# A list scheduler's order for a two-layer hybrid decoder: a table of leads by kind of work, and a model of TensorE's clock and of VectorE's waits for GpSimd

## The chip, the cores and the metric

One core of a Trainium2 chip runs the whole program. The time is device microseconds of one execution. The engines are TensorE (PE; its weight loads are shown apart as PEld), VectorE (DVE), ScalarE (ACT), GpSimd (POOL) and SyncE (SP), which issues the DMAs here. Each engine takes its instructions in a fixed order and waits on semaphores for the others.

## The reference

Two layers of a decoder trunk on 256 tokens of width 1024, all in float32:

```
for l in range(2):
    x = x + 0.5 * swiglu(rms_norm(x, ...), ...)        # 1024 -> 2816 -> 1024
    p = rms_norm(x, mix_norm[l]) @ w_in[l]             # columns split among three mixers
    ya = dsa_attention(...)       # indexer picks 64 of 256 keys per query, softmax over them
    yb = rwkv7_time_mix(...)      # delta-rule recurrence, 4 heads of 64
    yc = gated_deltanet(...)      # chunked gated delta rule, 4 heads of 64
    x = x + concat[ya, yb, yc] @ w_out[l]
    x = x + 0.5 * swiglu(rms_norm(x, ...), ...)
```

The weights are read once from HBM, some 180 MB.

## The kernel before

**Numbers.** A float32 product is made of three TensorE products of a rounded type: each weight tile `raw` (128x1024) comes by one DMA, ScalarE copies it to `hi`, VectorE subtracts to get `lo`, and the activations are split the same way (`xh`, `xl`; `hth`, `htl`; `yh`, `yl`). The products hi·hi, hi·lo and lo·hi add up in one PSUM bank `mm`. These are the *stream*; 2816-wide feed-forward parts and the projections consist of it. A *block* here is the run of matmuls that one weight unit gives one bank (6 of 512 columns, or 12 or 24 of 256). The mixers' own products are plain float32, are small, and go through banks called `tp` (and `po`). There are 8 PSUM banks in all, 6 of which may be `mm`; 3 `raw`, 7 `hi` and 7 `lo` buffers.

**Stages of a layer.** First feed-forward part; norm of both row tiles of 128 tokens (`norm`, L203: square on ScalarE, power on GpSimd, scaling `xn` on VectorE, transposes `tp<-per,xn` on TensorE, split to `xh`, `xl`); the mixers; the output projection (`down`, L227, whose last operands are `yh0`, `yl0` from the attention, while `yh1`, `yl1` come from the other two mixers); second feed-forward part.

**The mixers.** The projection's blocks (stream) feed three mixers, which run interleaved. The names that matter below: RWKV's `tile(t)` (L600) makes for each row tile and head one bank `tp<-ar,bk` (four matmul records of 64x256), of which VectorE makes `mb` (left half, L614) and `mk` (right half, L616): 16 such evictions in a layer, and a bank comes free only when both have been read. `inverse` (L390) inverts triangular matrices of 128 by steps on 32x32 blocks: `tp<-S,Mb` and `tp<-X,ST`, 64 records each, with an eviction to `X`, `S` or `ST` on VectorE or ScalarE behind each. `hb1` is RWKV's shifted projection, `vv` the delta net's convolution and `vm` the value residual of layer 1. `index` (L980) is attention's choice of keys (`wk`, `m8`), `soft` (L1036) its softmax, `o0` and `o1` are its outputs, and `y_out` (L477) transposes outputs and splits them to `yh`, `yl`.

**What sets the order.** The functions above do not emit the program. They only log it. `Plan` (L1152) cuts the log into groups (a block is one, a single instruction of the other engines is one), works out what depends on what, and gives each group a priority: its *tail*, the length of the longest chain from its start to the program's end, in estimated durations (`cost`, L1161) and hand-over times (`HOP`, L1132). `run` (L1278) then plays the program through: among all groups whose inputs are there and whose buffers are free, it takes the one that could start soonest, over all engines, and among those of one engine that could start at the same moment the one with the longest tail. The order in which groups are taken is the order in which `emit` writes them, on every engine. Nothing in the plan is a time on the chip; the engines start when their semaphores allow. SP's order of DMAs is fixed by the log.

Of the kernel before, what the change touches and what calls it, by code (L numbers as in the profile page):

```python
# [11 lines left out]
F32R = mybir.dt.float32r  # L12
AF = mybir.ActivationFunctionType
OP = mybir.AluOpType
# [3 lines left out]
D = 1024  # L18
# [75 lines left out]
class Log:  # L94
    def __init__(self, log, nc, engine):
        self.log, self.nc, self.engine = log, nc, engine
# [1033 lines left out]

PE, ACT, DVE, POOL, SP = [getattr(mybir.EngineType, n) for n in ("PE", "Activation", "DVE", "Pool", "SP")]
HOP = {PE: 210.0, ACT: 130.0, DVE: 115.0, POOL: 70.0, SP: 0.0}  # L1132
OWN = {PE: 0.0, ACT: 123.0, DVE: 104.0, POOL: 60.0, SP: 0.0}


# [12 lines left out]
def _cols(ap):  # L1148
    return math.prod(n for _, n in list(ap.ap)[1:])


class Plan:  # L1152
    def __init__(self, log, made, bias=lambda i: 0.0):
        self.log, self.made = log, made
        self.ins = [e[4] for e in log]
        self.eng = [i.engine for i in self.ins]
        self.graph()
        self.bundle()
        self.run([x + bias(k) for k, x in enumerate(self.tail)])

    def cost(self, i):  # L1161
        kind, e = type(i).__name__, i.engine
        aps = [a for a in list(i.outs) + list(i.ins) if hasattr(a, "bass_ap")]
        n = max(_cols(a) for a in aps)
        if kind == "InstDMACopy":
            return 400.0
        if e == PE:
            m = i.ins[0]
            n = _cols(m)
            if m.dtype == F32R:  # L1170
                return n * 0.4545
            if i.is_transpose:
                return n * 0.84
            k = list(m.ap)[0][1]
            return {32: 28.0, 64: max(107.0, n * 1.0)}.get(k, max(205.0, n * 1.67))
        if e == ACT:
            return 80.0 + n * 0.85 + 60.0 * (len(aps) > 2) + 200.0 * (len(aps) > 4) + 130.0 * (len(aps) == 3 and i.func == AF.Square)
        if e == POOL:
            if kind == "InstMemset":
                return 90.0 + n * 0.83  # L1180
            return 350.0 + n * 165.0 if getattr(i, "op", None) == OP.pow else 200.0 + n * 2.3
        fast = kind == "InstTensorScalarPtr" and len(aps) == 2
        slow = kind == "InstTensorScalarPtr" and len(aps) == 4
        if n == 129:
            return 600.0
        return 80.0 + 80.0 * (kind == "InstMax") + n * (0.52 if fast else 1.05) + 60.0 * slow

    def graph(self):
        hist, masks = {}, {}
        N = len(self.ins)  # L1190
        self.pred = [set() for _ in range(N)]
# [33 lines left out]
    def bundle(self):  # L1225
        N, last = len(self.ins), None
        node, group, same = [0] * N, [], None
        for k, i in enumerate(self.ins):
            key = None
            if self.eng[k] == PE:  # L1230
                key = [self.pair.get(a.bass_ap.tensor.name) for a in i.ins]
                key = max(x or "" for x in key)
                ap = i.outs[0].bass_ap
                to = (ap.tensor.name, ap.offset) if any(self.made[a.bass_ap.tensor.name][2] == "c1040" and a.dtype == F32R for a in i.ins) else None
            if key is not None and (key == last or to and to == same):
                group[-1].append(k)
            else:
                group.append([k])
                same = to if key is not None else None
            if key is not None and same != to:  # L1240
                same = None
            last = key
            node[k] = len(group) - 1
        self.group = group
        one = lambda l: [l[g[0]] for g in group]
        self.pred = [{node[p] for k in g for p in self.pred[k]} - {n} for n, g in enumerate(group)]
        self.dur = [sum(self.dur[k] for k in g) + (80.0 if self.eng[g[0]] == PE and not (self.ins[g[0]].ins[0].dtype == F32R) else 0.0) for g in group]
        self.use = [list(dict.fromkeys(u for k in g for u in self.use[k])) for g in group]
        self.left = {}
        for l in self.use:  # L1250
            for u in l:
                self.left[u] = self.left.get(u, 0) + 1
        self.eng, self.bytes = one(self.eng), one(self.bytes)
        self.table = [getattr(self.ins[g[0]], "func", None) for g in group]
        self.table = [None if f in (None, AF.Copy, AF.Square, AF.Relu, AF.Abs) else f == AF.Silu for f in self.table]
        N = len(group)

        sp = [k for k in range(N) if self.eng[k] == SP]
        for a, b in zip(sp, sp[1:]):
            self.pred[b].add(a)  # L1260
        for k in range(N):
            back = k - 1
            if back > 0 and (not self.pred[k] and self.eng[k] == POOL or
                             self.table[k] is not None and all(self.bytes[p] for p in self.pred[k])):
                self.pred[k].add(next(j for j in range(back, -1, -1) if self.eng[j] in (PE, ACT, DVE) or not j))
        self.succ = [[] for _ in range(N)]
        for k in range(N):
            for p in self.pred[k]:
                self.succ[p].append(k)
        self.tail = [0.0] * N  # L1270
        for k in reversed(range(N)):
            e, m = self.eng[k], 0.0
            for s in self.succ[k]:
                hop = 2300.0 + self.bytes[k] / 200.0 if self.bytes[k] > self.bytes[s] else OWN[e] if self.eng[s] == e else HOP[e]
                m = max(m, self.tail[s] + hop)
            self.tail[k] = m + self.dur[k]

    def run(self, prio):  # L1278
        N = len(self.eng)
        free = dict.fromkeys(HOP, 0.0)  # L1280
        ready = {e: [] for e in HOP}
        deg = [len(p) for p in self.pred]
        at = [0.0] * N
        kinds = lambda u: [self.made[u][2]] + (["mm"] if u[:3] == "mm_" else [])
# [7 lines left out]
        for _ in range(N):  # L1292
            best = None
            for e in HOP:
                for k in ready[e]:
                    t = max(free[e], at[k], fetch if many[k] > 7 else 0.0)
                    need = [g for u in self.use[k] if u not in self.slot for g in kinds(u)]
                    for g in set(need):
                        n = need.count(g)
                        t = max(t, sorted(spare[g])[n - 1][0] if n <= len(spare[g]) else math.inf)  # L1300
                    if self.table[k] not in (None, table):
                        t += 1300.0
                    c = (t, -prio[k], k)
                    if t < math.inf and (best is None or c[0] < best[0] or (c < best and self.eng[best[2]] == e)):
                        best = c
            assert best, "the plan is stuck"
            t, _, k = best
            e = self.eng[k]
            ready[e].remove(k)
            self.order.append(k)  # L1310
            table = table if self.table[k] is None else self.table[k]
            self.begin[k] = t
            for u in self.use[k]:
                if u not in self.slot:
                    self.slot[u] = [min(spare[g]) for g in kinds(u)]
                    for g, s in zip(kinds(u), self.slot[u]):
                        spare[g].remove(s)
            end = free[e] = t + self.dur[k]
            if many[k]:
                fetch = t + 60.0 * many[k]  # L1320
            if self.bytes[k]:
                dma = max(dma, t + 2300.0) + self.bytes[k] / 290.0
                end = dma
            for u in self.use[k]:
                left[u] -= 1
                if not left[u]:
                    for g, s in zip(kinds(u), self.slot[u]):
                        spare[g].append((end + HOP[e], s[1]))
            for s in self.succ[k]:
                at[s] = max(at[s], free[e] if self.bytes[s] and self.bytes[k] else end + (HOP[e] if self.eng[s] != e else OWN[e]))  # L1330
                deg[s] -= 1
                if not deg[s]:
                    ready[self.eng[s]].append(s)
        self.time = max(free.values())


    def emit(self, tc, dram):
# [118 lines left out]
```

## Time and profile before

| | |
|---|---|
| median of 3 runs | 1176.62 us (1176.09 to 1180.11) |
| profiled execution, its own time | 1178.08 us |
| its span, first to last instruction | 1176.3 us, 22847 instructions |
| busy: DVE, ACT, POOL | 764.2, 560.7, 114.7 us |
| mean granted TensorE clock | 0.978 |
| stages in the profiled span, about | layer 0: feed-forward 7 to 202, mixers and output projection 202 to 394, feed-forward to 587; layer 1: feed-forward to 776, mixers and output projection to 981, feed-forward to 1176 |

All instructions carry the line of `emit` (L1362), so the profile is read by tile names, not by lines. Buffers that several tiles share show as `c` in the profile and as `c` with a buffer's number in the order below. A matmul's end is modelled, so a busy TensorE may still be waiting in part, or run at half its clock; the column PEclk of the view by windows gives the granted clock in each stretch.

### The profile page before, as it was taken

Reading aid. Unit: us, or ns where it says so; the run is one execution under the profiler, and the core shown is the slowest. Engines: PE = TensorE matmul, PEld = TensorE weight load, DVE = VectorE, ACT = ScalarE, POOL = GpSimd, SP = SyncE. Lnnn points to the kernel's source line nnn. Section 1 sums busy time; section 2 is a strip of 40 time slices with the busy share of each in tenths; the row PEclk is TensorE's granted clock in tenths of the full one; section 3 lists DMA queues with packets and bytes.
Section 4 is the critical chain, followed back from the end, with each engine's and each line's share of the span. In section 5 each row is a group of like instructions: output and inputs, shape, how many; then the busy total and the mean of one; then the engine's idle time right before and its main releaser. Section 6 shows DMA issues by size and latency. Waiting matters only on the chain.

```text
span 1176.3 us, 22847 instructions
## 1 busy us (share of the span) xinstructions
PE 1134.6 (96%) x9508; PEld 1013.2 (86%) x9508; DVE 764.2 (65%) x1278; ACT 560.7 (48%) x855; POOL 114.7 (10%) x137
## 2 busy tenths in 40 slices
PE   7999999999998999999999999999699989999998
PEld 5999887987787799988889998879577877999887
DVE  5676545798786657664666674558957956576543
ACT  5554434565545445443454444447435454454431
POOL 0000001153141000000000000003321410000000
PEclk9999999999899999999999999999888999999999
DMA  7766556633232466655476665644321314666561
GB/s 235 222 194 192 183 193 192 179 107 94 73 96 67 118 205 180 183 193 189 152 218 177 191 185 191 214 134 144 96 86 38 109 54 127 197 182 192 183 194 56
DMA packets 96998, 182.76 MB, mean 155 GB/s; under 512 B 9856, under 2 KB 36608, under 8 KB 96896
## 3 DMA queue, kind: packets, MB, share of 16 engines
q1 hardware_dynamic: 96752, 181.25, 51.2%
q8 instruction: 74, 1.21, 0.4%
q14 instruction: 28, 0.23, 0.1%
q10 hardware_dynamic: 144, 0.07, 0.0%
HBM read 180.25 MB, written 1.05 MB: 154 GB/s over the span
## 4 chain that ended last, share of the span: by engine, by line
PE 82%; DVE 10%; ACT 4%; issue 1%; DMA 1%; POOL 0%; SPq 0%; ACTq 0%; DVEq 0%; POOLq 0%
PE mm L1362 75%; PE tp L1362 7%; DVE c L1362 5%; DVE lo L1362 2%; ACT s L1362 1%; ACT hi L1362 1%; ACT c L1362 1%; PE po L1362 1%; DVE hb L1362 1%; DMA gb<-in_ffn_norm 0%; DMA raw<-in_w_in 0%; DVE s L1362 0%; POOL c L1362 0%; ACT xh L1362 0%; DVE bdt L1362 0%
## 5 line engine op out<-in xcount | busy, mean ns | idle before, releaser
L1362 DVE TENSOR_TENSOR lo<-raw,hi 128x1024 fp32r<-128x1024 f32 (+2 forms) x332 | 407.5, 1228 | 303.0 <-ACT hi L1362 302.1
L1362 ACT CAST hi<-raw 128x1024 fp32r<-128x1024 f32 (+2 forms) x332 | 347.1, 1047 | 412.7 <-PE mm L1362 341.8
L1362 PE MATMUL mm<-xh,hi 128*128 128x256 f32 x1360 | 384.6, 283 | 0.0
L1362 PE MATMUL mm<-xh,lo 128*128 128x256 f32 x1360 | 382.9, 282 | 0.8 <-DVE lo L1362 0.8
L1362 PE MATMUL mm<-xl,hi 128*128 128x256 f32 x1360 | 382.6, 281 | 0.0
L1362 PEld LDWEIGHTS mm<-xh,hi 128*128 128x128 f32 x1360 | 256.4, 189 | 1.9 <-issue 1.0
L1362 PEld LDWEIGHTS mm<-xl,hi 128*128 128x128 f32 x1360 | 256.6, 189 | 0.8 <-issue 0.2
L1362 PEld LDWEIGHTS mm<-xh,lo 128*128 128x128 f32 x1360 | 256.2, 188 | 1.2 <-DVE lo L1362 1.2
L1362 PE MATMUL mm<-hi,htl 128*128 128x512 f32 x352 | 138.7, 394 | 0.0
L1362 PE MATMUL mm<-lo,hth 128*128 128x512 f32 x352 | 138.5, 393 | 0.0
L1362 PE MATMUL mm<-hi,hth 128*128 128x512 f32 x352 | 138.4, 393 | 0.0
L1362 POOL TENSOR_TENSOR c<-c,per 128x256 f32<-128x256 f32 (+7 forms) x66 | 67.9, 1042 | 433.1 <-DVE c L1362 346.6
L1362 PE MATMUL mm<-hi,xh 128*128 128x512 f32 (+2 forms) x256 | 103.5, 404 | 0.7 <-ACT xh L1362 0.4
L1362 PE MATMUL mm<-hi,xl 128*128 128x512 f32 (+2 forms) x256 | 99.0, 387 | 4.9 <-DVE xl L1362 4.9
L1362 PE MATMUL mm<-lo,xh 128*128 128x512 f32 (+2 forms) x256 | 98.5, 385 | 0.5 <-DVE lo L1362 0.5
L1362 PEld LDWEIGHTS mm<-hi,htl 128*128 128x128 f32 x352 | 66.0, 188 | 15.4
L1362 PEld LDWEIGHTS mm<-lo,hth 128*128 128x128 f32 x352 | 66.1, 188 | 15.0
L1362 PEld LDWEIGHTS mm<-hi,hth 128*128 128x128 f32 x352 | 66.2, 188 | 14.8
L1362 PEld LDWEIGHTS mm<-hi,xl 128*128 128x128 f32 x256 | 50.6, 198 | 15.7 <-DVE xl L1362 6.7
L1362 PEld LDWEIGHTS tp<-c,c 32*32 32x32 f32 (+2 forms) x2328 | 41.2, 118 | 25.7 <-issue 19.8
L1362 PE MATMUL tp<-c,c 32*32 32x32 f32 (+3 forms) x2328 | 50.5, 210 | 11.3 <-DVE mk L1362 8.7
L1362 PEld LDWEIGHTS mm<-hi,xh 128*128 128x128 f32 x256 | 51.0, 199 | 11.6 <-issue 1.7
(160 smaller groups left out, 1137.3 us busy)
## 6 DMA issues: line engine op xcount, KB each, us to landing
raw<-in_ffn_w_gate SPq DMA_DIRECT2D x88, 512.0 KB, 3.8
raw<-in_ffn_w_up SPq DMA_DIRECT2D x88, 512.0 KB, 3.8
raw<-in_ffn_w_down SPq DMA_DIRECT2D x88, 512.0 KB, 3.6
raw<-in_w_in SPq DMA_DIRECT2D x46, 512.0 KB, 3.8
raw<-in_w_out SPq DMA_DIRECT2D x16, 512.0 KB, 3.4
gb<-in_ffn_norm SPq DMA_DIRECT2D x4, 512.0 KB, 4.5
raw<-in_w_in SPq DMA_DIRECT2D x4, 384.0 KB, 6.7
pp<-in_params SPq DMA_DIRECT2D x2, 729.5 KB, 6.8
```

What stands on the lines that cost most here:

```text
L1362: ins = getattr(getattr(nc, engine), op)(*map(real, a), **{n: real(x) for n, x in kw.items()}).ins
```

## The change

The reference's arithmetic, the log and the dependences stay as they are: 3144 groups before and after, and SP's order is the same in every place. What changes is how `run` chooses:

- A table `AHEAD` of 159 kinds of group (named by the tiles written and read) is added to the tail, in the plan's microseconds: `"mk0<-tp,per": 4.1` lets such a group go as if its chain were 4.1 us longer.
- An engine no longer takes only the group that could start soonest: all that could start within `SOON` of that (150 ns on PE, 200 on ACT, 100 on DVE and POOL) compete by priority.
- A model of TensorE's clock: windows of 3413 ns, beginning at a fixed phase of 0 from the plan's start, in which matmul activity is added up; after a window with too little (0.18 of full activity when warm, 0.25 when cold) the next runs at 0.53 of the speed.
- VectorE's one-input forms (`fast`) wait in the plan until GpSimd is done; other forms do not.
- 120 ns when TensorE goes from the stream to a plain float32 product, and a higher cost for wide GpSimd work.

```diff
+SOON = {PE: 150.0, ACT: 200.0, DVE: 100.0, POOL: 100.0, SP: 0.0}
+AHEAD = {
+    "D<-mb0": -7.0, "D<-mb1": -4.7, "D<-mg0": -1.9, "D<-mg1": 0.2, "Mb<-D,per": -11.6, "S64<-": 2.2, "S64<-S": -35.0,
...
+WINDOW, COLD, WARM, PHASE = 3413.0, 0.25, 0.18, 0.0
...
-        self.run([x + bias(k) for k, x in enumerate(self.tail)])
+        self.run([x + 1e3 * AHEAD.get(self.kind(k), 0.0) for k, x in enumerate(self.tail)])
...
+        def clock(t):
+            w = int((t + PHASE) // WINDOW)
+            while len(warm) <= w:
+                warm.append(used.get(len(warm) - 1, 0.0) >= (COLD if warm[-1] else WARM))
+            return w, warm[w]
...
+                    if e == PE and was and not self.stream[k]:
+                        t += 120.0
+                    if self.fast[k] and free[POOL] - pool < t:
+                        t = max(t, free[POOL])
...
-                    c = (t, -prio[k], k)
-                    if t < math.inf and (best is None or c[0] < best[0] or (c < best and self.eng[best[2]] == e)):
+                    if t < math.inf:
+                        can.append((t, -prio[k], k))
+                if can:
+                    soon = min(can)[0] + SOON[e]
+                    c = min((c for c in can if c[0] <= soon), key=lambda c: c[1:])
+                    if best is None or c[0] < best[0]:
                         best = c
```

At another place in their engine's order than before stand 305 of 644 groups on PE, 398 of 794 on ACT, 86 of 133 on POOL and 724 of 1214 on DVE, moved by at most 42 places. Three places show what moved.

**VectorE, layer 1, RWKV's evictions.** Before, these rows stand between the last but one `mb` of the second row tile and its last; `c_7_769` is `vv`, `c_8_802` its tanh:

```order
L1362 SCALAR_TENSOR_TENSOR hb_7449<-pb_7128,pp_1558,hb_7449 128x256
L1362 SCALAR_TENSOR_TENSOR c_7_769<-c_0_273,c_3_3738,c_7_769 128x256 x4
L1362 TENSOR_TENSOR lo_105<-raw_72,hi_100 128x1024
L1362 SCALAR_TENSOR_TENSOR c_7_769<-c_0_273,c_3_3738,c_7_769 128x256 x2
L1362 TENSOR_TENSOR lo_217<-raw_69,hi_209 128x1024
L1362 TENSOR_TENSOR vm<-per_61,hb_7449 128x512
L1362 SCALAR_TENSOR_TENSOR c_7_769<-c_8_802,c_7_769 128x512
L1362 TENSOR_TENSOR lo_169<-raw_67,hi_156 128x1024
L1362 TENSOR_TENSOR mk_7968<-tp,per_61 128x256 x4
```

Now all evictions of both row tiles stand in one run, with one weight split among them:

```order
L1457 SCALAR_TENSOR_TENSOR mb_7854<-tp,c_7_1897,per_61 128x256 x2
L1457 TENSOR_TENSOR mk_7872<-tp,per_61 128x256
L1457 SCALAR_TENSOR_TENSOR mb_7854<-tp,c_7_1897,per_61 128x256
L1457 TENSOR_TENSOR mk_7872<-tp,per_61 128x256 x2
L1457 SCALAR_TENSOR_TENSOR mb_7854<-tp,c_7_1897,per_61 128x256
L1457 SCALAR_TENSOR_TENSOR mb_7888<-tp,c_7_1897,per_61 128x256
L1457 TENSOR_TENSOR mk_7872<-tp,per_61 128x256
L1457 SCALAR_TENSOR_TENSOR mb_7888<-tp,c_7_1897,per_61 128x256
L1457 TENSOR_TENSOR mk_7907<-tp,per_61 128x256 x2
L1457 SCALAR_TENSOR_TENSOR mb_7888<-tp,c_7_1897,per_61 128x256
L1457 TENSOR_TENSOR lo_196<-raw_67,hi_187 128x1024
```

The rows of `hb`, `vv`, `vm` and the splits that stood ahead of the first `mk` now come behind the evictions, among the steps of `inverse`.

**TensorE, layer 1, end of the mixers.** `yh_9235` and `yl_9247` are the other mixers' operands of the output projection, `yh_9433` and `yl_9435` attention's, and `c_5_566` is attention's output of row tile 0. Before:

```order
L1362 MATMUL mm<-hi_209,yh_9235 128x512
L1362 MATMUL mm<-lo_217,yh_9235 128x512
L1362 MATMUL mm<-hi_209,yl_9247 128x512
L1362 MATMUL tp<-per_61,c_5_566 128x128 x4
L1362 MATMUL mm<-hi_156,yh_9433 128x512
L1362 MATMUL mm<-lo_169,yh_9433 128x512
```

Now (`c_6_767` and `c_8_802` are attention's two outputs, `yh_9213` the other mixers' operand):

```order
L1457 MATMUL tp<-per_61,c_5_2367 128x128 x2
L1457 MATMUL tp<-per_61,c_6_767 128x128 x4
L1457 MATMUL tp<-per_61,c_8_802 128x128 x4
L1457 MATMUL mm<-hi_107,yh_9213 128x512
L1457 MATMUL mm<-lo_118,yh_9213 128x512
L1457 MATMUL mm<-hi_107,yl_9223 128x512
```

Before, attention's output of row tile 0 is transposed right ahead of the blocks that need it. Now the last block of the other mixers' operand (12 matmuls) stands between; in layer 0 this place is as before.

**TensorE, start of the program.** The transposes of the second row tile's `xn`, and the second weight unit's block (`hi_107`, `lo_118`). Before:

```order
L1362 MATMUL mm<-hi_107,xh_96 128x512
L1362 MATMUL mm<-lo_118,xh_96 128x512
L1362 MATMUL mm<-hi_107,xl_102 128x512
L1362 MATMUL tp<-per_61,xn 128x128 x8
L1362 MATMUL tp<-c_1_149,per_61 128x128
L1362 MATMUL mm<-hi_135,xh_96 128x512
```

Now:

```order
L1457 MATMUL mm<-hi_98,xh_96 128x512
L1457 MATMUL mm<-lo_105,xh_96 128x512
L1457 MATMUL mm<-hi_98,xl_100 128x512
L1457 MATMUL tp<-per_61,xn 128x128 x8
L1457 MATMUL mm<-hi_107,xh_96 128x512
L1457 MATMUL mm<-lo_118,xh_96 128x512
```

The block of the second unit went from ahead of these transposes to behind them.

More of the change, by code (lines that the diff above doesn't have):

```diff
@@ L1132 @@
 HOP = {PE: 210.0, ACT: 130.0, DVE: 115.0, POOL: 70.0, SP: 0.0}
+SOON = {PE: 150.0, ACT: 200.0, DVE: 100.0, POOL: 100.0, SP: 0.0}
+AHEAD = {
+    "D<-mb0": -7.0, "D<-mb1": -4.7, "D<-mg0": -1.9, "D<-mg1": 0.2, "Mb<-D,per": -11.6, "S64<-": 2.2, "S64<-S": -35.0,
+    "S64<-tp": 4.1, "S<-ST": -0.5, "ST<-D,per": 0.7, "ST<-tp": -1.2, "X<-tp": 24.4, "X<-tp,per": -3.0,
+    "ar<-kx,cc": 0.4, "ast<-ast": -12.1, "ba<-mm": -19.0, "bdt<-ST": -1.3, "bdt<-tp": -0.7, "bk<-bk,e1": 17.8,
+    "bk<-kx,e1": -11.5, "bk<-kx,wa": 0.2, "cc<-cc": 19.1, "cc<-wa,cc,per": 37.9, "cw<-pp": -16.8,
+    "dd0<-dd0,per": 14.3, "dd0<-tp": 1.2, "dd1<-dd1,per": 0.3, "de1<-per,sp": 1.0, "dg<-per,ss": 17.9,
+    "ea<-pp": 43.6, "eg<-tp": -1.1, "gR<-tp,neg,gvt": -0.3, "gkt<-tp,kc": 10.8, "gr<-gr": -5.8, "gr<-mm,rsb": 14.2,
+    "gsq<-qk": -14.6, "gss<-gs2": 1.2, "gu<-gu,zo": 2.2, "gu<-qz,tp": -1.2, "gu<-tp": 15.3, "gvt<-tp,nr": 0.6,
+    "gw<-gw,rg": 27.7, "gw<-rg,pp": -13.5, "gw<-vt,rb": 13.8, "gzb<-tp,per": -0.5, "hb1<-hb1,vm": -36.2,
+    "hb1<-pb1,om": 0.4, "hp<-pp": 0.2, "hth<-tp": -11.0, "htl<-tp,hth": 62.9, "kT<-tp": 0.3, "kbt<-tp": 1.5,
+    "kbt<-tp,rb": 1.4, "kr<-kr": -1.7, "kr<-kr,kss": -6.7, "kr<-kr,ktm": -11.7, "kr<-kv1,per": 17.8,
+    "kr<-kv1,rt": 5.4, "kss<-kss": -0.8, "kss<-kss,per": 26.4, "kss<-ktm": -4.8, "ktm<-kv0": 10.7,
[3 rows of a table added]
+    "nr<-nr": -31.8, "nr<-tp": -4.0, "o1<-po,ast": 3.0, "om<-pp": 1.0, "out<-per": 3.4, "pT0<-tp": 0.3,
+    "pb1<-": -1.6, "per<-hb1": 15.9, "per<-mm,per": 12.2, "pg1<-": -2.7, "qT0<-tp": 36.9, "qT1<-tp": -11.8,
+    "qiT0<-tp": -19.8, "qk<-pg0,cw": 0.8, "qr<-q,per": -3.8, "qr<-qr,tm": -0.8, "qs<-qs": -5.7,
+    "qss<-qss,per": -25.8, "rW<-tp": 4.0, "rb<-tp": -3.6, "rf<-wa": 4.3, "rg<-tp": -9.9, "rmv<-rmv": 15.4,
+    "rmv<-rmv,per": 0.2, "rt<-per,pp": 8.1, "ry<-ry,gw": 2.0, "s0,ast<-s0,ast,qss": 0.7, "sg<-mm,ss": -0.3,
+    "sg<-mm,ss,sg": -1.4, "sp<-ba": -2.4, "sp<-ba,pp": 23.1, "sp<-sp,ea": 23.0, "th<-qk": -0.7, "tm<-q": 9.2,
+    "tm<-q,per": 5.3, "tm<-q,rt": 4.9, "tp<-S64,mb0": 0.7, "tp<-X64,bdt": 16.0, "tp<-ar,bk": -3.8,
+    "tp<-de0,per": -18.6, "tp<-de1,per": 4.1, "tp<-dg,per": -1.1, "tp<-gzb,qk": 1.1, "tp<-kT,qT1": 67.3,
+    "tp<-per,bk": 0.4, "tp<-per,gsq": -0.1, "tp<-per,hb1": -5.3, "tp<-per,kr": 2.7, "tp<-per,o0": -0.6,
+    "tp<-per,o1": -31.1, "tp<-per,s0": -3.5, "tp<-per,s1": -11.1, "tp<-per,sg": -0.8, "tp<-per,sq": 30.7,
+    "tp<-per,vv": -0.6, "tp<-per,xn": 0.9, "tp<-pp,lt": -1.6, "ur<-mm,rsb": -22.2, "ur<-ur,gr": -12.0, "vd<-tp": 1.0,
+    "vm<-tp,hp": -14.4, "vm<-vm": -0.3, "vt<-tp": -12.8, "vv<-pg1,cw,vv": -37.8, "vv<-th,vv": -4.8, "wi<-kv1": -37.1,
[3 rows of a table added]
+}
@@ L1152, with __init__ @@
 class Plan:
-    def __init__(self, log, made, bias=lambda i: 0.0):
+    def __init__(self, log, made):
         self.log, self.made = log, made
@@ L1158, in __init__, with kind @@
         self.bundle()
-        self.run([x + bias(k) for k, x in enumerate(self.tail)])
+        self.run([x + 1e3 * AHEAD.get(self.kind(k), 0.0) for k, x in enumerate(self.tail)])
+    def kind(self, n):
+        i = self.ins[self.group[n][0]]
+        names = [[a.bass_ap.tensor.name.rstrip("0123456789").removesuffix("_") for a in l if hasattr(a, "bass_ap")] for l in (i.outs, i.ins)]
+        return ",".join(names[0]) + "<-" + ",".join(dict.fromkeys(names[1]))
     def cost(self, i):
@@ L1180, in cost @@
                 return 90.0 + n * 0.83
-            return 350.0 + n * 165.0 if getattr(i, "op", None) == OP.pow else 200.0 + n * 2.3
+            return 350.0 + n * 165.0 if getattr(i, "op", None) == OP.pow else 200.0 + n * (2.3 if n < 512 else 3.0)
         fast = kind == "InstTensorScalarPtr" and len(aps) == 2
@@ L1253, in bundle @@
         self.eng, self.bytes = one(self.eng), one(self.bytes)
+        self.fast = [self.eng[n] == DVE and type(self.ins[g[0]]).__name__ == "InstTensorScalarPtr" and
+                     sum(hasattr(a, "bass_ap") for a in list(self.ins[g[0]].ins) + list(self.ins[g[0]].outs)) == 2 or
+                     self.eng[n] == DVE and type(self.ins[g[0]]).__name__ == "InstTensorCopy" for n, g in enumerate(group)]
+        self.act = [0.0] * len(group)
+        for n, g in enumerate(group):
+            if self.eng[n] == PE:
+                for k in g:
+                    m, w = self.ins[k].ins[0], self.ins[k].ins[1]
+                    two = 1 if m.dtype == F32R or self.ins[k].is_transpose else 2
+                    self.act[n] += two * _cols(m) * list(m.ap)[0][1] * _cols(w) / 16384 / 8192
+        self.stream = [self.eng[n] == PE and self.ins[g[0]].ins[0].dtype == F32R for n, g in enumerate(group)]
+        self.alt = [0.0] * len(group)
+        for n, g in enumerate(group):
+            i = self.ins[g[0]]
+            kinds = [self.made.get(a.bass_ap.tensor.name, "--x")[2] for a in list(i.ins) + list(i.outs) if hasattr(a, "bass_ap")]
+            if i.engine == DVE and type(i).__name__ == "InstTensorTensor" and "ps" not in kinds:
+                w = max(_cols(a) for a in i.outs)
+                if w >= 256:
+                    self.alt[n] = 200.0 + w * 2.3
         self.table = [getattr(self.ins[g[0]], "func", None) for g in group]
@@ L1279, in run, with done @@
         N = len(self.eng)
+        was, pool = None, 0.0
+        used, warm = {}, [True]
+        def clock(t):
[3 more added lines that the diff above has]
+            return w, warm[w]
+        def done(n, t):
+            left = self.dur[n]
+            while left > 0.01:
+                w, full = clock(t)
+                v = 1.0 if full else 0.53
+                d = min(left, max(0.02, (w + 1) * WINDOW - PHASE - t) * v)
+                used[w] = used.get(w, 0.0) + self.act[n] * d / self.dur[n]
+                left -= d
+                t += d / v
+            return t
         free = dict.fromkeys(HOP, 0.0)
@@ L1294, in run @@
             for e in HOP:
+                can = []
                 for k in ready[e]:
@@ L1317, in run @@
                         spare[g].remove(s)
-            end = free[e] = t + self.dur[k]
+            was = self.stream[k] if e == PE else was
+            end = free[e] = done(k, t) if e == PE else t + self.dur[k]
+            pool = self.dur[k] if e == POOL else pool
             if many[k]:
@@ L1334, in run @@
         self.time = max(free.values())
+        self.cold = sum(not x for x in warm)
     def emit(self, tc, dram):
```

6 rows, old and new, of the table AHEAD are left out of this document.

## The prediction

> **What bounds the kernel now.** I read the page's totals first, then the stretches of the span with their granted clock, then TensorE's waits, then the chain that ended last.
>
> ```profile
> PE 1134.6 (96%) x9508; PEld 1013.2 (86%) x9508; DVE 764.2 (65%) x1278; ACT 560.7 (48%) x855; POOL 114.7 (10%) x137
> ...
> 60.00:120.00 60.00, 60.00 (x509) 60.00 (x508) 39.48 (x44) 27.75 (x32) 0.00 (x0) 1.00 0.67 193
> ...
> 253.00:291.00 38.00, 35.70 (x815) 29.42 (x815) 34.74 (x74) 17.71 (x38) 14.22 (x13) 1.00 0.28 83
> ...
> 827.00:865.00 38.00, 29.01 (x352) 23.00 (x352) 29.68 (x64) 13.64 (x30) 11.60 (x10) 0.78 0.33 98
> 865.00:887.00 22.00, 22.00 (x761) 16.32 (x749) 15.18 (x26) 11.78 (x22) 5.76 (x6) 1.00 0.31 100
> ```
>
> TensorE is busy 96% of the span, and in a feed-forward part (60 to 120) all of it at the full clock. The order changes nothing of its work, so only two things can be won: its waits (1176.3 − 1134.6 = 42 us, of which the first 7.5 us are the input's way in), and stretches at a lower granted clock. The mean clock in the table above, 0.978, is what some 52 us at 0.5 give (0.022 × 1176 / 0.5). The fourth row stands out: in layer 1, from 827 to 865, TensorE is busy 29 of 38 us, and the clock is 0.78. TensorE's waits from 820 to 1000 name the cause:
>
> ```profile
> PE tp L1362 <- DVE mk L1362: 8.7, 1, 8.7
> ...
> PE mm L1362 <- ACT yh L1362: 1.2, 1, 1.2
> PE mm L1362 <- DVE yl L1362: 0.6, 1, 0.6
> ```
>
> One wait of 8.7 us is the longest in the program behind the start. The chain that ended last, followed through that place, shows what VectorE did meanwhile:
>
> ```profile
> 845.54 0.39 DVE hb L1362
> 845.93 1.58 DVE c L1362 x4
> 847.51 0.07 DVE lo L1362
> 847.58 0.99 issue
> 848.57 0.87 DVE c L1362 x2
> 849.44 1.14 DVE lo L1362
> 850.58 0.60 DVE vm L1362
> 851.17 0.60 DVE c L1362
> 851.78 1.14 DVE lo L1362
> 852.91 0.35 DVE mk L1362
> ```
>
> From 845.5 to 852.9 VectorE works on `hb1`, `vv`, `vm` and three splits that TensorE needs much later, while banks of `tp<-ar,bk` stay full because their `mk` half is not read. Only after the first `mk` does TensorE go on. Layer 0 has no such wait. The windows of low clock lie where TensorE idles or does small products:
>
> ```profile
> 827.43:830.85 3.42, 3.42 (x16) 3.10 (x16) 3.42 (x7) 0.62 (x2) 1.00 (x1) 0.50 0.00 0
> 847.92:861.58 13.66, 8.19 (x141) 6.02 (x142) 10.86 (x25) 2.19 (x6) 1.78 (x2) 0.50 0.40 118
> 892.30:902.54 10.24, 10.24 (x176) 8.10 (x175) 6.26 (x23) 4.26 (x9) 1.59 (x3) 0.50 0.01 2
> 305.21:315.45 10.24, 10.24 (x177) 8.04 (x176) 6.23 (x23) 4.04 (x8) 1.58 (x3) 0.50 0.02 3
> 967.39:970.81 3.42, 3.42 (x9) 2.68 (x10) 0.00 (x0) 0.00 (x0) 0.00 (x0) 0.50 0.52 153
> ```
>
> **The change, part by part.**
>
> *1. The evictions of layer 1.* All `mb` and `mk` now stand in one run, with one split among them; a bank is read within a few instructions of 0.4 us. The wait of 8.7 us goes. What is late next is VectorE itself, since the work that stood ahead of `mk` is not gone: it now lies among the steps of `inverse`. I counted the changed order from RWKV's last product but one to the `tp<-X,ST` near the end of the second row tile's 32x32 steps. TensorE has 3 blocks of 12 and 8 of 6 matmuls, 13 steps of 64 records and 9 small groups. VectorE has 66 instructions, 8 of them splits.
>
> ```profile
> 842.20:872.00 29.80, 20.91 (x482) 14.95 (x482) 20.11 (x42) 9.12 (x18) 8.91 (x11) 0.77 0.27 84
> ...
> L1362 DVE TENSOR_TENSOR lo<-raw,hi 128x1024 fp32r<-128x1024 f32 x4 | 4.8, 1206 | 0.0
> ...
> 862.53 0.68 PE tp L1362 x50
> 863.22 1.59 PE mm L1362 x6
> ```
>
> In the first row VectorE has 42 instructions in 20.11 us; without the 4 splits (second row) 38 in 15.3, or 0.40 each. So the counted VectorE work is 8 × 1.21 + 58 × 0.40 = 33 us. TensorE's is 11 blocks of about 1.5 and 13 steps of 0.68, 25 us, and I estimate 8 us for the 9 small groups, whose rows are from 0.2 to 2: 33 us as well. With no slack a VectorE that is busy 91% of the time, as in 253 to 291 (34.74 of 38), takes 33 / 0.91 = 36.5 us, and TensorE waits some 4 us. At 100% it would wait nothing, at 85% 6 us. I take 4: **−8.7 + 4 = −4.7 us**, between −8.7 and −2.7.
>
> *2. The clock behind that wait.* From 853.4 on work runs at half clock:
>
> ```profile
> 842.25 1.13 PE L1362 MATMUL tp<-ar,bk 64*128 64x256 f32 x4
> ...
> 854.40 2.07 PE L1362 MATMUL tp<-ar,bk 64*128 64x256 f32 x4
> ...
> 853.39 3.08 PE tp L1362 x68
> 856.47 2.86 PE mm L1362 x6
> 859.33 1.01 PE tp L1362 x64
> 860.34 2.19 PE mm L1362 x6
> ```
>
> Against the full-clock rows (1.13, 1.59, 0.68) these lose 0.9 + 1.3 + 0.3 + 0.6, and the step that the 3.08 us at 853.4 begin with (3.08 − 2.07 = 1.01 against 0.68) another 0.3: **−3.4 us**, if the low clock came from the wait; 0 if another low stretch takes its place.
>
> *3. Other low windows.* 892 to 902 costs at most half of 10.24 us; counted by step and block it is about 4. Eight small groups follow each other there before a stream block comes; in the changed order never more than six, in either layer. I take half in layer 1, **−2.0**, and nothing in layer 0 (305 to 315), where the runs of small groups are of nearly the old lengths. The window at 827 (at most 1.7) follows the two reductions with two columns, which stand together there. The change parts them in layer 1 and puts them together in layer 0: −1.0 and +0.5, **−0.5**.
>
> *4. The end of layer 1's mixers.* A block of 12 matmuls now lies between the last transposes and the blocks that need `yh0`, and covers the waits of 1.2 and 0.6 us quoted above; the window at 967 behind them costs at most 1.7. Against it, two blocks that covered the softmax's hand-overs have moved ahead of it. **−1.5**, between −3.5 and +1.
>
> *5. The start.*
>
> ```profile
> 13.79 0.63 PE L1362 MATMUL mm<-hi,xh 128*128 128x512 f32 x1
> ...
> 15.54 0.40 PE L1362 MATMUL mm<-hi,xl 128*128 128x512 f32 x1
> 15.78 1.04 PE L1362 MATMUL tp<-per,xn 128*128 128x128 f32 x8
> ```
>
> The second unit's block fills 13.79 to 15.78 while the transposes wait for `xn`. Behind them it costs its full-clock time, 6 × 0.24, less a small product moved away: **+1.2 us**; up to +3 if the clock is then released a window later (the matmuls of 0.63 are the slow ones).
>
> *6. Heads of the two mixers.* With the second row tile's transposes side by side its splits begin earlier.
>
> ```profile
> PE mm L1362 <- DVE xl L1362: 4.9, 5, 1.5
> ```
>
> Five such waits make 4.9 us in the program; I take a sixth off, **−0.8**. Elsewhere engines other than TensorE are reordered under a TensorE that is busy all of the time, and that covers them; if the cover went, a late split would cost up to its 1.2 us.
>
> Sum: −4.7 − 3.4 − 2.0 − 0.5 − 1.5 + 1.2 − 0.8 = −11.7. The profiled execution took 1178.08 us (span 1176.3 and 1.8 around it), which makes 1166.4; it lies 1.5 above the median of the runs, 1176.62, so for the median I say **1165 us**.
>
> [...] The granted-clock rows come in 3.42, 10.24 and 13.66 us: one, three and four windows of 3.41. [...]
>
> ```profile
> 841.61 3.40 POOL L1362 TENSOR_TENSOR c<-c,per 128x256 f32<-128x256 f32 x4 [6.98 <-ACT c L1362]
> ...
> 842.72 0.83 DVE L1362 SCALAR_TENSOR_TENSOR hb<-pb,pp,hb 128x256 f32<-128x256 f32 x1 [0.73 <-ACT hb L1362]
> ...
> 845.46 0.47 DVE L1362 SCALAR_TENSOR_TENSOR hb<-pb,pp,hb 128x256 f32<-128x256 f32 x1
> ```
>
> Beside GpSimd's work the same VectorE operation takes 0.83 us instead of 0.47, though it has two tensor inputs, a form for which the new plan books no wait. [...]
>
> **Rivals.** *The low clock comes back elsewhere.* For it: small products fill the steps of `inverse` whatever their order, and low windows are there in both layers. Against it: the largest followed the 8.7 us wait. Parts 2 and 3 are nil and half of 4: −4.7 − 0.7 + 1.2 − 0.8 = −5: 1172. *All low windows of the mixers go.* Then the other half of 892, the 4 us at 305 and a window's 1.7 come off as well: −7.7 more, 1157. *The change doesn't do what it says*: other gaps open and eat it: 1176.6. *Slower: VectorE's queue holds up `inverse`.* The mechanism is in part 1: the 33 us. In 865 to 887 VectorE was busy 15.18 of 22, 69%, waiting on others' results; at 70% the 33 us take 47, TensorE waits 14 instead of 8.7, the low windows stay, and the start and layer 0's window add 1.7, the heads give 0.8: +6.3, 1183. It decides below a share of some 78% (33 / 0.78 = 42, a wait of 9). Against it: TensorE was never short of work in that stretch, so VectorE's idle time there did no harm, and where VectorE was the one waited for it reached 91%.
>
> **How the numbers follow.** Chances: forecast 0.55 (1159 to 1170), clock elsewhere 0.18, all low windows gone 0.12, nothing won 0.08, slower 0.07. The range 1154 to 1175 takes in the first three and leaves out the last two and a little at the lower end. 0.5%, 5.9 us, is about what a measurement of this kernel can tell from no change; 1170.7 is the limit. Faster: 0.55 + 0.12 + a third of 0.18 = 0.73. Slower: 0.07. The same: 0.20.
>
> **What would show it.** No wait of TensorE for `mk` over 1 us and full clock where the first `tp<-S,Mb` of layer 1 follow: parts 1 and 2. VectorE over 90% busy and TensorE's waits for `X`, `S` or `ST` up to 4 us together in the steps of layer 1: the remainder of part 1. No wait for `yh0` in layer 1, and 1.2 us in layer 0: part 4. The transposes at 15.8 with TensorE idle ahead of them: part 5. The forecast is wrong if low windows in both layers sum to 50 us again, or if TensorE's waits in layer 1 do not fall.

## The result and the profile after

| | before | changed |
|---|---|---|
| median of the runs taken together | 1178.36 us (4 runs) | 1158.98 us (4 runs, 1156.39 to 1162.02) |
| ratio | | 0.9839, 95% interval 0.9809 to 0.987 |
| profiled execution: own time, span | 1178.08, 1176.3 us | 1156.39, 1154.6 us |
| mean granted TensorE clock | 0.978 | 0.996 |

The change made the kernel 19.4 us faster; 11.7 were forecast. A run over 1.5% above the fastest of its kernel counts as slow and is left out of the ratios and of what follows from spans and clocks; that is one run of all, in e1_mk_lead. The page of the changed kernel, its totals:

```profile
PE 1120.0 (97%) x9508; PEld 1000.5 (87%) x9508; DVE 763.0 (66%) x1278; ACT 560.3 (49%) x855; POOL 120.3 (10%) x137
```

Of the 21.7 us between the two profiled spans, TensorE's busy time lost 14.6 (1134.6 to 1120.0) with the same 9508 matmuls, and its idle time 7.1 (41.7 to 34.6). The work is the same, so I put the 14.6 down to the clock. The view by windows shows what is left of low clock (us, then busy time and count of PE, PEld, DVE, ACT, POOL, granted clock, DMA share, GB/s), and the place that was at 0.78 before:

```profile
243.45:246.86 3.41, 3.41 (x12) 1.63 (x12) 2.74 (x9) 3.41 (x10) 0.00 (x0) 0.50 0.81 288
304.89:308.30 3.41, 3.41 (x72) 3.02 (x69) 3.15 (x13) 0.81 (x2) 0.00 (x0) 0.50 0.02 5
820.30:823.71 3.41, 3.41 (x18) 2.69 (x15) 3.41 (x7) 1.27 (x2) 0.00 (x0) 0.50 0.00 0
...
844.00:870.00 26.00, 20.44 (x631) 15.51 (x617) 24.42 (x41) 15.50 (x28) 10.56 (x10) 1.00 0.44 130
870.00:895.00 25.00, 24.47 (x649) 19.67 (x649) 20.82 (x57) 14.63 (x32) 3.32 (x4) 1.00 0.18 61
```

Three windows, 10.2 us, stand where 51.2 us stood. What stood ahead of the old ones differs. Of the eight stretches of low clock before, five follow a window of 3.41 us in which TensorE was busy for less than half: the three below, the one ahead of 779.67 (busy 1.47 us) and the one in the wait for `mk` (0.21 us):

```profile
202.82:206.23 3.41, 1.32 (x7) 0.72 (x6) 3.41 (x5) 2.91 (x6) 0.40 (x1) 1.00 0.15 25
376.90:380.31 3.41, 1.58 (x7) 0.85 (x6) 1.83 (x2) 1.44 (x2) 0.00 (x0) 1.00 0.07 6
963.99:967.40 3.41, 1.58 (x9) 0.83 (x8) 1.83 (x2) 1.53 (x2) 0.00 (x0) 1.00 0.00 0
```

The first is the head of the mixers (waits for `xn`, `xh` and `xl`), the other two are the ends of the mixers (waits for `yh0` and `yl0`). The other three (305, 827, 892) follow windows in which TensorE was busy 2.5 to 2.8 us, with small products. In the changed kernel no window behind the start is busy for less than half, and the three that are left follow windows busy 2.84 to 3.41 us. So low clock follows two kinds of window here, those that TensorE mostly idles through (busy 0.2 to 1.6 us) and busy ones with small products (2.5 to 3.4 us), and the change took from both. In layer 1 the steps of `inverse` (844 to 895) run at the full clock from end to end, although TensorE idles 5.6 of the first 26 us. There VectorE is the bound: busy 24.42 of 26, 94%. TensorE's waits in the same stretch, 800 to 965 (us in total, times, longest):

```profile
PE tp L1457 <- DVE c L1457: 3.8, 4, 1.7
PE tp L1457 <- ACT c L1457: 1.9, 3, 1.1
PE tp L1457 <- POOL c L1457: 1.0, 1, 1.0
```

No wait for `mk` and none for `yh` is among them. The chain that ended last passes the place as before, and is VectorE's again:

```profile
844.75 1.77 DVE lo L1457
846.52 0.95 DVE c L1457 x2
847.48 0.19 issue
847.66 0.49 DVE c L1457 x2
848.15 0.99 issue
849.14 1.76 DVE lo L1457
850.91 0.88 DVE hb L1457
```

The two splits take 1.77 and 1.76 us, where they took 1.14 in the chain of before. In the view by time, GpSimd works without a break beside them, and the next split, behind that work, is short again:

```profile
844.46 7.04 POOL L1457 TENSOR_TENSOR c<-c,per 128x256 f32<-128x256 f32 x6 [0.91 <-ACT c L1457]
```

```profile
853.43 1.08 DVE lo L1457
```

### The profile page after: what moved, and what is told of

The parts are those of the page before. It is cut to its first block, busy times and chain, and to the rows that moved or that the text cites. A ratio compares the mean times of both kernels' runs of the same rounds, so it can differ in the third digit from the quotient of the medians.

```text
span 1154.6 us, 22833 instructions
## 1 busy us (share of the span) xinstructions
PE 1120.0 (97%) x9508; PEld 1000.5 (87%) x9508; DVE 763.0 (66%) x1278; ACT 560.3 (49%) x855; POOL 120.3 (10%) x137
## 3 DMA queue, kind: packets, MB, share of 16 engines
q8 instruction: 74, 1.21, 0.4%
## 4 chain that ended last, share of the span: by engine, by line
PE 80%; DVE 11%; ACT 3%; DMA 2%; issue 2%; POOL 1%; SPq 0%; ACTq 0%; DVEq 0%; POOLq 0%
PE mm L1457 73%; PE tp L1457 7%; DVE c L1457 4%; DVE lo L1457 3%; ACT hi L1457 1%; DMA raw<-in_ffn_w_gate 1%; ACT c L1457 1%; PE po L1457 1%; POOL c L1457 1%; DMA raw<-in_w_in 1%; ACT s L1457 1%; DVE qk L1457 1%; DVE xn L1457 1%; DMA gb<-in_ffn_norm 0%; DMA raw<-in_ffn_w_up 0%
## 5 line engine op out<-in xcount | busy, mean ns | idle before, releaser
L1457 POOL TENSOR_TENSOR c<-c,per 128x256 f32<-128x256 f32 (+7 forms) x66 | 74.2, 1139 | 429.4 <-DVE c L1457 333.2
L1457 PE MATMUL mm<-hi,xh 128*128 128x512 f32 (+2 forms) x256 | 100.4, 392 | 0.3 <-ACT hi L1457 0.3
L1457 PE MATMUL mm<-hi,xl 128*128 128x512 f32 (+2 forms) x256 | 96.4, 377 | 3.0 <-DVE xl L1457 3.0
L1457 PE MATMUL mm<-lo,xh 128*128 128x512 f32 (+2 forms) x256 | 95.8, 374 | 0.5 <-DVE lo L1457 0.5
```

What stands on the lines that cost most here:

```text
L1457: ins = getattr(getattr(nc, engine), op)(*map(real, a), **{n: real(x) for n, x in kw.items()}).ins
```

## The experiments

Three theories. **A**: the granted clock follows how densely wide products, those of the stream above all, lie among the small ones; the new order spreads the stream's blocks better. **B**: low clock only follows a long wait of TensorE; the lost `mk` wait is the whole gain. **C**: the plan's model of the clock steers the order past low windows.

Each run lists its span and mean clock. The low clock of a run, as used below, is (1 − clock) × span / 0.5; 0.50 is the clock of all eight low stretches before and all three after.

### The evictions alone: e1_mk_lead

The old kernel and rule, with two kinds led by 40:

```diff
+AHEAD = {"mk0<-tp,per": 40.0, "mk1<-tp,per": 40.0}
-        self.run([x + bias(k) for k, x in enumerate(self.tail)])
+        self.run([x + 1e3 * AHEAD.get(self.kind(k), 0.0) for k, x in enumerate(self.tail)])
```

> The kernel before, with a lead of 40 us for the mk evictions alone; old rule of choice, no model. Theory A (the granted clock follows how many stream blocks stand among the small products): the wait of 8.7 us goes and with it the low clock right behind it, but some 20 to 28 us of low clock stay in the 32x32 steps of both layers, mean clock 0.984 to 0.988; about 1166 us. Theory B (the low clock of layer 1 all follows from the long wait): layer 1 has at most one low window, clock 0.99 or more, about 1160 us, as much as the whole change.

Measured: 1165.11 us (1152.89 to 1176.69), ratio 0.9869 (0.9805 to 0.9934). The four runs of this one order:

| span | clock | low clock |
|---|---|---|
| 1151.1 | 0.997 | 7 us |
| 1160.5 | 0.987 | 30 us |
| 1166.1 | 0.979 | 49 us |
| 1174.9 (the one left out) | 0.972 | 66 us |

TensorE's waits in the profiled one, the fastest, hold no wait for `mk`; these are the first two:

```profile
PE tp L1370 <- DVE xn L1370: 9.5, 5, 7.4
PE mm L1370 <- DVE xl L1370: 4.8, 5, 1.5
```

The long wait is gone, and one of the other runs has as much low clock (49 us) as the kernel before (42 to 66). So B does not hold as it stands: the wait can have been one cause of low clock, not the only one. And the three faster runs of the same order lie 15 us apart by their clock alone, 0.36 us of span for each us of low clock (15.0 / 42.1).

At 7 us of low clock this order spans 1151.1 us, and the changed kernel at 7 to 9 us 1153.8 to 1154.9. TensorE idles 34.1 us in the one (1151.1 − 1117.0) and 34.6 in the other. So a lead for the two `mk` kinds alone already gives all that the change wins in waits; what the change has over it is that it keeps the clock more often (14 us of low clock on the mean of ten runs, against 29 of three).

### The table under the old rule: e2_table_old_rule

Before's `run` and costs with the whole of `AHEAD` added to the tail, nothing else.

> The kernel before with the whole table of leads, but the old rule of choice and no model of clock, GpSimd or switching. Theory A (the table spreads blocks among the steps, and that alone keeps the clock): clock 0.99 or more, VectorE's bound in layer 1 a little worse than after the change (I count 5 us where the change has 3.5), 1160 to 1163 us. Theory C (the clock model places the work): low windows of 25 us or more return, about 1170 us.

Measured: 1161.11 us (1159.51 to 1164.15), ratio 0.9878 (0.9846 to 0.9911), clock 0.986 to 0.991, which is 21 to 33 us of low clock. The time is A's; the clock is only in part at A's 0.99 or more, and some runs have the 25 us of C. The table alone gives most of the change's gain, 14.8 us beside the kernel before (1175.88).

### The models without the table: e3_model_no_table

```diff
-AHEAD = {
...
+AHEAD = {}
```

> The changed kernel with an empty table: new rule of choice and all models, priorities are the bare tails. Theory A: in layer 0 about 13 us of small products follow each other without a stream block and VectorE's queue holds TensorE up by some 10 us there, so a wait and low clock in layer 0, layer 1 clean; about 1170 us. Theory C: the model keeps the clock at 0.99 or more and the time is within 4 us of the changed kernel's 1159.

Measured: 1187.13 us, ratio 1.0103 (1.0061 to 1.0144): slower than before, and slower than any theory had it. Two stretches of its view by windows, one in each layer, and two of TensorE's waits:

```profile
256.39:276.87 20.48, 16.83 (x218) 12.04 (x222) 17.58 (x47) 6.49 (x19) 10.58 (x9) 0.50 0.17 53
840.07:857.14 17.07, 15.88 (x47) 11.91 (x47) 13.57 (x36) 4.81 (x14) 6.49 (x7) 0.50 0.21 62
```

```profile
PE tp L1427 <- ACT c L1427: 5.0, 4, 2.2
PE mm L1427 <- ACT c L1427: 4.4, 1, 4.4
```

A plan that models the clock, with the new rule of choice, made more low clock (69 to 95 us a run) than one that does not know of it. C falls.

### The change without the plan's clock: e4_no_clock, e4_again

```diff
-                v = 1.0 if full else 0.53
+                v = 1.0
```

> The changed kernel with the plan's clock always at full speed, the table as it is. Order in the 32x32 steps is nearly the changed kernel's. Theory A: clock 0.992 or more and 1158 to 1163 us, so the clock model itself is worth under 4 us. Theory C: 25 us or more of low clock return, about 1167 us or more.

Measured: 1156.47 us (1153.08 to 1159.45), ratio 0.983 (0.9798 to 0.9861). Run again beside the changed kernel on one chip:

> The kernel of the run e4_no_clock, word for word, beside the changed kernel on the same chip. If the plan's clock gives nothing and costs the 1 us at the start, it is 1 to 3 us below the changed kernel; if the earlier 1156.5 was chance, the two agree within 1 us.

> The changed kernel, word for word, again and with more runs. Both theories: median 1157 to 1161. If the low clock differs from run to run because the chip's windows start at a phase of their own, then the spans of the single runs lie on one line with their clocks, some 0.4 us of span for each us of low clock.

Measured: e4_again 1157.89 us (0.9834, 0.9813 to 0.9856), the changed kernel 1157.62 us (0.9851, 0.9818 to 0.9885). So the 1156.5 was chance, and the model of the clock, whose limits for a window are the plan's own and are tested by no run here, gives nothing that can be measured. Nor does it show a cost at the start. In the view of one tile by time, the transposes of the first mixers' norm begin at 202.3 us in the kernel before, at 203.4 and 202.6 in the two profiled executions of the changed one, and at 201.7 and 202.4 in those without the plan's clock (count, then shortest, median and longest in ns, first and last start; one fence for each kernel, in this order):

```profile
L1362 PE MATMUL tp<-per,xn x8: 272/273/328, 202.3 to 203.8; 128*128 128x128 f32 x8
```

```profile
L1457 PE MATMUL tp<-per,xn x8: 272/273/329, 203.4 to 204.9; 128*128 128x128 f32 x8
...
L1457 PE MATMUL tp<-per,xn x8: 273/273/328, 202.6 to 204.2; 128*128 128x128 f32 x8
```

```profile
L1457 PE MATMUL tp<-per,xn x10: 271/272/302, 201.7 to 206.0; 128*128 128x128 f32 x10
...
L1457 PE MATMUL tp<-per,xn x8: 272/273/302, 202.4 to 204.1; 128*128 128x128 f32 x8
```

Executions of one kernel differ by 0.7 to 0.8 us here. In the later pair, where the last matmul of 128x512 at the start that takes 0.63 us begins at 16.10 and at 15.92, the two kernels are 0.2 us apart. The 203.4 has two waits between 28 and 46 us in it that the other execution of the same kernel has not:

```profile
PE mm L1457 <- ACT c L1457: 0.7, 1, 0.7
PE mm L1457 <- DVE c L1457: 0.5, 1, 0.5
```

The second execution of the changed kernel that was profiled has its low windows at other places:

```profile
303.36:306.77 3.41, 3.15 (x72) 2.87 (x72) 2.85 (x11) 1.22 (x4) 0.00 (x0) 0.50 0.02 5
825.60:829.01 3.41, 3.41 (x10) 2.54 (x8) 2.52 (x13) 0.93 (x4) 1.55 (x2) 0.50 0.86 254
```

On a grid of 3.413 us from the first instruction (the 10.24 us of low clock at 305.21 before, over 3), a window of the first execution begins at a remainder of 1.1 us (304.89) and of the second at 3.0 (303.36). The phase is another one in these two executions of one kernel, so a plan with the one phase of 0 can meet it only by chance.

### No long wait, but bare steps: e8_mk_late

The changed kernel with `mk` held back in the table:

```diff
-    "mk0<-tp,per": 4.1
+    "mk0<-tp,per": -30.0, "mk1<-tp,per": -30.0
```

> The changed kernel with mk0 and mk1 given -30 in the table instead of 4.1 and nothing. In its order VectorE never stands in front of a step of layer 1 by more than some 6 us of work, so no single wait is as long as the old 8.7, but TensorE's small products stand in runs of 8 to 10 us without a stream block in both layers (3.6 to 4.8 in the changed kernel). Theory A (the granted clock follows how many stream blocks lie among the small products): low clock of 30 us or more, mean clock 0.987 or less, median 1164 to 1170. Theory B (low clock only follows a long wait): as the changed kernel, low clock under 16 us, clock 0.993 or more, median 1157 to 1161. Theory C (the plan's model of the clock avoids low windows; it is still in): as B.

Measured: 1183.42 us, ratio 1.0066 (1.0042 to 1.0091), low clock 61 to 81 us in five runs: twice the 30 us that A asks for, and slower than its 1164 to 1170. TensorE's waits in layer 0's mixers (250 to 340), all of them, and the window ahead of the longest low stretch and that stretch itself:

```profile
PE tp L1457 <- ACT c L1457: 1.6, 2, 1.1
PE mm L1457 <- ACT c L1457: 1.1, 1, 1.1
PE tp L1457 <- DVE mk L1457: 0.3, 1, 0.3
```

```profile
300.56:303.97 3.41, 2.84 (x36) 2.26 (x35) 2.73 (x9) 1.98 (x6) 0.00 (x0) 1.00 0.17 66
303.97:334.69 30.72, 30.72 (x356) 26.73 (x353) 15.68 (x44) 9.59 (x21) 0.00 (x0) 0.50 0.06 19
```

The same two of the tile `mm` alone, which is the stream (us, then PE, PEld, DVE, ACT):

```profile
300.56:303.97 3.41, 1.01 (x5) 0.49 (x3) 0.00 (x0) 0.00 (x0) 1.00 0.17 66
303.97:334.69 30.72, 8.74 (x18) 5.55 (x18) 0.00 (x0) 0.00 (x0) 0.50 0.06 19
```

Nine windows of half clock in a row, TensorE busy all of the time, and no wait over 1.1 us in the stage. What is missing is the stream: 18 matmuls of it in 30.72 us. In this stage A holds and B does not. Layer 1's long stretch at half clock, 870.58 to 891.06, tells less: TensorE idles 8.1 of its 20.48 us. In layer 0's stretch the low clock came with no wait over 1.1 us, so here short waits were not enough to keep the clock.

### The blocks used up early: e10_bare_steps

The changed kernel without the plan's clock, and the stream led:

```diff
+    "mm<-hi,xh": 10.0,
```

> The changed kernel without the plan's clock, and with a lead of 10 for the stream blocks of hi and xh: the blocks are used up early in the mixers, and the steps of inverse then stand in one run of 37 us in layer 0 and 40 us in layer 1 without a stream block. Theory A: most of both runs at half clock, 50 us or more of low clock in all, mean clock 0.978 or less, and with some waits more a median of 1172 to 1195. Theory B: no low clock there unless a single wait over 6 us comes ahead of it; clock 0.99 or more, median 1157 to 1166.

Measured: 1197.83 us (A had 1172 to 1195), ratio 1.0181 (1.0156 to 1.0206), low clock 62 to 96 us, as A has it. Three stretches of the tile `mm` alone:

```profile
331.02:348.09 17.07, 0.00 (x0) 0.00 (x0) 0.00 (x0) 0.00 (x0) 0.50 0.00 1
911.29:935.18 23.89, 0.00 (x0) 0.00 (x0) 0.00 (x0) 0.00 (x0) 0.50 0.21 68
...
348.09:365.15 17.06, 0.00 (x0) 0.00 (x0) 0.00 (x0) 0.00 (x0) 1.00 0.01 1
```

All three are without the stream, and only two are at half clock; the third follows the first at once. The groups of instructions of TensorE in the window ahead of the first (327.61 to 331.02, at full clock and busy all of the time), the four costliest, show what stood ahead of the fall:

```profile
L1458 PE MATMUL tp<-c,c 32*32 32x32 f32 x32 | 1.4, 192 | 0.0
L1458 PE MATMUL tp<-c,c 64*128 64x128 f32 x8 | 0.7, 297 | 0.0
L1458 PE MATMUL tp<-c,mb 64*64 64x64 f32 x8 | 0.7, 224 | 0.0
L1458 PE MATMUL tp<-c,mg 64*64 64x64 f32 x4 | 0.5, 243 | 0.0
```

And in the third stretch, which kept the full clock, though TensorE was busy only 14.12 of its 17.06 us:

```profile
L1458 PE MATMUL tp<-c,mk 128*128 128x64 f32 x24 | 4.0, 264 | 0.0
L1458 PE MATMUL tp<-c,mb 128*128 128x64 f32 x16 | 3.1, 275 | 0.0
L1458 PE MATMUL tp<-c,bdt 128*128 128x64 f32 x16 | 2.2, 278 | 0.0
L1458 PE MATMUL tp<-c,ar 128*128 128x128 f32 x8 | 1.8, 308 | 0.5 <-ACT c L1458 0.5
```

In the one, products on 32 or 64 rows make nearly the whole of the window; in the other, products over all 128 rows make most of the stretch. So A has to be put more narrowly. The stream itself is not needed for the full clock: the third stretch has none of it for 17.06 us. And TensorE being busy is not enough: it was busy 3.41 of 3.41 us ahead of the first fall, and 3.12 ahead of the second (907.88 to 911.29, again mostly products on 32 or 64 rows). My estimate from these rows is that the kind of work in a window counts, and that the narrow products count for little; no run changes that alone, and where the limit lies the runs do not tell. The five windows of the kernel before that were less than half busy (0.2 to 1.6 of 3.41 us) fit it too: they are its only ones at full clock behind the start, and half clock followed all of them.

### Other numbers in the table: e12_spread_a, e13_spread_b

The kernel of e4_no_clock with some 215 numbers of `AHEAD` changed or added, among them, in e13_spread_b:

```diff
-    "Mb<-D,per": -11.6, "hb1<-hb1,vm": -36.2, "mb1<-tp,rb,per": -6.8,
...
+    "Mb<-D,per": -23.9, "hb1<-hb1,vm": -32.2, "mb1<-tp,rb,per": -10.3, "tp<-S64,mb1": 5.7,
...
```

> The kernel of e4_no_clock with other numbers in the table (214 kinds differ), chosen by two rules taken from the runs so far: let no step of TensorE's small products stand behind VectorE's queue, and leave no longer stretch of small products between stream blocks than 4 to 5 us where they are narrow. In its order the longest that VectorE's work stands ahead of a small product in layer 1's inverse is about 5 us (6 in e4_no_clock, 10 before). Theory A: low clock of 25 us or less, mean clock 0.990 or more, 1 to 8 us under the changed kernel: 1150 to 1157. If what is left is chance of the windows' phase, the same as e4_no_clock: 1156 to 1158.

> As e12_spread_a with a second set of numbers (221 kinds differ from the changed kernel's): in its order no small product of layer 1's inverse stands behind more than 3 us of VectorE's work, and the narrow stretches are 4 to 5 us. The changed kernel's TensorE idles 5.6 of 26 us there, with VectorE busy 94%. If that idle time goes and the low clock stays at 25 us or less: 1146 to 1154. If the waits merely move to another engine: 1155 to 1160. If the stretches of 4 to 5 us already cost the clock: 1160 or more.

Measured: 1147.32 us (1146.29 to 1147.53), ratio 0.9756 (0.9741 to 0.9771), and 1147.23 us (1144.69 to 1148.98), ratio 0.9755 (0.9737 to 0.9773). By the ratios both beat the changed kernel by some 10 us; the first is 3 us under A's 1150 to 1157, the second lies in its 1146 to 1154. The totals of e13_spread_b, and the first 26 us of the steps of `inverse` in layer 1:

```profile
PE 1120.5 (98%) x9508; PEld 1002.3 (88%) x9508; DVE 763.3 (67%) x1278; ACT 563.2 (49%) x855; POOL 113.1 (10%) x137
```

```profile
834.50:860.50 26.00, 23.43 (x756) 17.05 (x743) 23.19 (x43) 12.79 (x25) 6.23 (x8) 1.00 0.39 124
```

TensorE idles 2.6 us there instead of 5.6; GpSimd is busy for 6.23 us instead of 10.56, which may be why, but no run changes that alone. In the whole program TensorE's busy time is that of the changed kernel, and its idle time 24.9 us (1145.4 − 1120.5) instead of 34.6. The low clock of the eight runs is 9 to 18 us (mean 17, beside 14 in the changed kernel). So these 10 us are waits.

## Why the prediction was right, and where its sizes were not

**Its bound and its mechanism held.** TensorE is busy 97%, and both things that could be won were won. Taken by its steps:

*1, the wait for `mk`, −4.7.* (33 / 0.91 is 36.3 and not 36.5, so the wait left by that sum was 3.3 us rather than 4.) The wait is gone, and VectorE is late next, as foretold: 94% busy (over 90% was the mark). TensorE idles 5.6 us in the first half of the steps where I had 4; my 1.21 us for a split is too short for those that stand beside GpSimd's work (1.77). All waits of the program together fell by 7.1; parts 1, 4 and 6 had 7.0, an agreement that is in part luck, since part 4 has some clock in it.

*2 and 3, the clock, −5.9 together.* Here the size failed. All of the low clock at 848 to 862 and 892 to 903 is gone, where I took off half of the second; layer 0's, at which I put nothing, went from 10.24 to 3.41; and the windows at 206, 380 and 780, another 10.2 us that the sum does not name at all, are gone in both profiled executions of the changed kernel. The last three are those behind TensorE's waits at the heads and the end of the mixers, so a part of what I booked as short waits also carried low clock. In runs: the kernel before has 52 us of low clock on the mean (42 to 66 in 27 runs), the changed one 14 (7 to 35 in 10). Within the kernels of this study, 75 runs of 10 orders, a us of low clock goes with 0.35 us of span. So the clock's share is (52 − 14) × 0.35 = 13 us, and 4 of the 17.3 between the mean spans (1174.8 and 1157.5) are left to the waits and the start; the profiled pair has it as 14.6 and 7.1. The outcome, 1158.98, lies between the forecast and the rival by which all low windows of the mixers go (1157), nearer to the rival.

The step that failed is the count "in the changed order never more than six" small groups in a row. It was used for layer 1 alone and at half its worth, though layer 0's longest run in the steps falls from eight to six as well. And it holds for the steps of `inverse` only: at the end of the mixers the changed order has 25 small groups in a row in layer 0, and 15 and 14 in layer 1, which run at the full clock. So it is not the number of groups that decides; the groups that stood ahead of a fall in e10 are the narrow ones (32 and 64 rows).

*The two reductions of part 3.* Put together in layer 0, they run at 251.5 to 254.9 in the profiled execution (250.4 to 253.8 in the other), and no low clock follows in either; the window at 243.45 was over before them. Parted in layer 1, the first of them, at 818.0 to 819.7, has the window at 820.30 right behind it. So neither the −1.0 nor the +0.5 came, and whether they stand together did not decide it in these two executions.

*4, the end of layer 1's mixers, −1.5.* The waits for `yh0` and `yl0` and the window at 967 are gone in layer 1; in layer 0 the wait stays:

```profile
PE mm L1457 <- ACT yh L1457: 1.2, 1, 1.2
```

From the first product with `yh0` (965.87 and 946.80) to the transposes of the next norm (982.3 and 960.6) it was 16.4 us and is 13.8: −2.6, and −3.8 with the wait of 1.2 us that stood ahead of it. I took −1.5, and −3.5 at most.

*5, the start, +1.2.* From 202.3 to 203.4 it is +1.1, but that it agrees is luck: at the hundredth matmul the changed kernel is only 0.2 us late (33.00 against 32.78), most of the rest are the waits between 28 and 46 us, and in its other execution the place is at 202.6. The transposes did not stay at 15.8 with TensorE idle ahead of them; they run from 13.91 on, right behind the first block, where TensorE is still slow: the eight take 1.48 us there and took 1.04 at 15.78 before, and the matmuls of 128x512 ahead of them take 0.63 us, those from 15.46 on 0.40.

*6, the heads, −0.8.* The waits for `xl` fell from 4.9 to 3.0 us, but those for `xn` rose from 9.6 to 10.2: −1.3. Right in kind.

**The phase of the windows.** The plan's model has one phase, and two executions had two (remainders of 1.1 and 3.0 us). Parts 2 and 3 did not need it: the order has less low clock in every one of its ten runs (7 to 35 us, 14 on the mean) than the kernel before in any of 27 (42 to 66, mean 52).

**The rivals.** "The low clock comes back elsewhere" is what two of e1's runs (30 and 49 us) and e8 look like; it did not happen to this order. "VectorE's queue holds up `inverse`" had its mechanism (VectorE at 94%, 5.6 us of waiting) and not its price: the share stayed far above 78%.

**Still open.** Which of the 159 entries keep the clock; what in a window decides; what the new rule of choice, the wait for GpSimd and the 120 ns give beside the table (e2_table_old_rule has 26 us of low clock on the mean and e4_no_clock 18, with some 4 us between their spans); and why the new rule without the table is 11 us slower than the old one, beyond the low stretches shown.

## What to carry to other kernels

Where small products run between blocks of large ones, spread the blocks and read the granted clock of each stretch: with 18 stream matmuls in 30.72 us all of that time was at half clock (e8). An order that shortens waits and bares such a stretch can lose more than it gains (e3: the longest wait behind the start 4.4 us instead of 8.7, TensorE idle 40.4 us in all instead of 41.7, and slower than before). Read the granted clock of several executions before crediting an edit with a few us: one order had from 7 to 49 us of low clock in three runs. And when the clock is whole again, go back to the waits: there were 10 us more in them.

## What the runs showed of the hardware

- TensorE busy all of the time ran at half clock for 30.72 us (e8), and idling 5.6 of 26 us it kept the full clock (the changed kernel). But behind each of the five windows of 3.41 us in which it was busy for less than half in the kernel before (0.2 to 1.6 us), the clock fell to 0.50.
- Low clock came in pieces of 3.41 us (3.41, 10.24 and 13.66 us in the kernel before), on a grid whose phase differed between two executions of the changed kernel (remainders 1.1 and 3.0 us). The spread of one kernel's runs goes mostly with it (correlation of span and low clock within kernels 0.93).
- A us of low clock cost 0.35 us of span (75 runs of 10 orders), not 0.5. Products slowed down by less than twice: a step of 64 records took 0.68 us at full clock and 1.01 at half, a block of six stream matmuls 1.59 and 2.86. And part of the low clock fell where TensorE idled (5.5 of the 13.66 us at 847.92 before).
